# Weight preparation, two adaLN dots and a planned order around the output projection of an encoder layer

## The chip, the cores and the metric

The kernel runs on one core of one Trainium2 chip. The metric is the device time of one execution in microseconds, the median of several runs. Matmuls run on PE (TensorE, its weight loads are PEld), elementwise work on DVE (VectorE) and ACT (ScalarE), a few powers on POOL (GpSimd). SP (SyncE) issues nearly all loads from memory, and POOL issues the stores.

## The reference, cut to what matters

One layer, 1024 positions, 1024 channels, all in float32:

```python
mod = silu(c) @ w_ada + b_ada
sh1, sc1, gt1, sh2, sc2, gt2 = split(mod, 6)
h = rmsnorm(x, norm1_g) * (1 + sc1) + sh1
u, v, q, k, va, gate_a, gate_b = split(h @ w_in, cuts)
a_out = gmlp_branch(u, v, ...) @ w_a              # per chunk of 128 positions
b_out = window_attention_branch(q, k, va, ...) @ w_b
merged = sigmoid(gate_a) * a_out + sigmoid(gate_b) * b_out
x = x + gt1 * (merged @ w_o)
h2 = rmsnorm(x, norm2_g) * (1 + sc2) + sh2
f_gate, f_up = split(h2 @ w_ffn_in, 2)
x = x + gt2 * ((silu(f_gate) * f_up) @ w_ffn_out)
```

## The kernel before, in words

**Numbers.** Each float32 operand of a large product is kept as a high and a low part. A product is the sum of three products of parts (high x high, high x low, low x high). For a weight unit of 128 x 1024 a load fills a `raw` tile, ACT casts it to the high part `wh` and DVE subtracts to get the low part `wl`. `wpool` has three buffers each of `raw`, `wh` and `wl`, so the load of a unit waits until the unit three before it is no longer read. Helper functions record every operation of an engine, so nearly all rows of the profile have line 144; loads have L198 and stores L203 or L206. Rows are told apart by tile names.

**Stages.** `half(0)` and `half(1)` (L643) handle 512 positions each: q and k of the attention, v, the gMLP branch, and then a loop d = 0 to 7 over output channels with `w_a` and `w_b` (units `w_ab[d]`). `gate_products` (L1389) computes gates and `merged`, for d = 2 to 7 in a form with seven products of half the size (Strassen's), in the order of `STEPS` (L1376). `out_products` (L1518) does the product with `w_o` in the same form, adds it to x, and forms column sums of squares for the second norm. The FFN follows.

**The conditioning vector.** A row of w_ada is 512 KB, loaded as a 128 x 1024 tile. `ada_late` (L604) is one dot of it with silu(c) on DVE; after each fourth column a few small operations on `mod`. In half 0, `ada_next(2)` (L1231) does two dots in each of d = 2 and d = 3. Their tiles come out of `raw`. While half 0 runs, its loop also squares half 1's x (`sumsq`, two rows per d, on ACT with a sum into `ss` on DVE), and at the loop's d = 4 PE reads `ss` for the column sums (`col_rstd`, L374). In half 1's loop over k for q and k (L854), `ada_late` is called as often as a table of eight numbers says, on rows that `ada_load` (L629) loaded in pairs into a `mid` tile one or more k earlier. `mid` tiles rotate over eight buffers; the stores of `hd` (half 1's modulated x) read some of them.

**The gates' end.** For d = 7, steps 4 and 5 of `gate_products` also cast and split the first two units of `w_o`. The products of `out_products` need token blocks with names T1, T2, T3, T4, B11, B21, B22: sums of quarters of `merged`, each as high part (ACT) and low part (DVE), in four rows k of 128 x 512. T1 is the quarter `x0`, whose sums are done by d = 5; its four casts and four low parts were the second thing that `out_products` issued.

**A planned order.** `out_products` does not issue its work as written. Each `add` records an operation with its engine, a cost, and the names that it reads and writes, in a `Plan` (L42). `order` simulates the engines, takes at each step the operation that can start first, and then the one due earliest, and issues all operations sorted by simulated start. V is DVE, A is ACT, T is PE, D is SP's loads, G is POOL's stores. PE's and SP's order is the order of `add`; V, A and G are free within the dependencies. `free` is when each engine is taken to come free at the start:

```python
now = {e: free.get(e, 0.0) for e in queues}
...
key = (max(at, now[e] + 0.3), late[i], i)
...
plan.run({"V": 2.5, "A": 1.5, "T": 0.0})
```

**The products with w_o.** Output rows are treated in four pairs p. Each product of a pair is 12 matmuls of 512 columns. `USE` (L1615) says which weight unit and block each takes: M1 and M2 take `w_o[2p]` itself (key "0", blocks B11 and B21); T2 and T3 take a unit A of sums of w_o, T1 and B22 a unit C of sums, both from a scratch `sO` in memory in two parts; T4 takes halves of odd rows of w_o (unit B). First come all M1 and M2 (L1688), then T2, T3, T4 (L1727), then T1 and B22 (L1794). M1, T2, T3 and T4 of a pair accumulate in one PSUM bank, and between them `accumulate` (L1634) lets DVE read that bank into a row of the result. Where `(name, p)` is in `THROUGH`, ACT copies the scaled bank to a tile `t`, and DVE adds that from SBUF. `need` (L1605) and `make` (L1583) fetch, cast and split a unit; `fetch` (L1572) plans the load. `col_sums` (L1760) is behind the first T1. Two units for the FFN, `w_gate[4]` and `w_gate[5]` ("f", 0 and 1, tiles `first`), are loaded and prepared on the way.

Of the kernel before, what the change touches and what calls it, by code (L numbers as in the profile page):

```python
# [19 lines left out]
KT = D // P  # L20
# [86 lines left out]
def kernel(  # L107
# [535 lines left out]
    def half(hf):  # L643
# [102 lines left out]
        for k in range(KT):  # L746
# [97 lines left out]
            if hf == 1:  # L844

                if k in (0, 2, 4):
                    wq_raw = raw_unit(w_q[k // 2 + 1])
                if k == 2:
                    wk_raw = raw_unit(w_kv[1])
                if k == 4:  # L850
                    wk = unit(None, V, wk_raw)
                if k in (1, 3, 5):
                    wq_next = unit(None, V, wq_raw)
                for _ in range((0, 2, 2, 2, 2, 3, 3, 0)[k]):  # L854
                    ada_late(*ada_loaded.pop(0), silu_c)
                if k < 6:
                    ada_load()
# [304 lines left out]
        for d in range(KT):  # L1162
# [65 lines left out]
            if d == 4:  # L1228
                h_next.extend([[hid(), hid()], [hid(), hid()]])
            if d in (2, 3):  # L1230
                ada_next(2)  # L1231
# [157 lines left out]
    def gate_products(hH, hL):  # L1389
# [30 lines left out]
        def ready_sum(f, n):  # L1420
# [4 lines left out]
            if n == 3:  # L1425
                for i, q in enumerate((a11, a22, a12, a21)):
                    store(sF[f][:, i * HALF : (i + 1) * HALF], q)

        for d in GD:
            banks = {}  # L1430
            for i, (u, part, t, b, first) in enumerate(STEPS):
# [40 lines left out]
                if d == KT - 1:  # L1472
                    if i == 2:
                        mH, mL = [hid(), hid()], [hid(), hid()]
                    if i in (2, 3, 5):
                        for k in ((0, 1), (2, 3, 4), (), (5, 6))[i - 2]:
                            split(merged[0][k // 4][:, k % 4, :], mH[k // 4][:, k % 4, :],
                                  mL[k // 4][:, k % 4, :])
                    if i == 4:
                        oblk["T1"] = (fpt("tt1h"), fpt("tt1l"))  # L1480
                        wo_units.append(unit(w_o[0]))
                    if i == 5:
                        wo_units.append(unit(w_o[2]))
                if (d, i) == (GD[0], 5):
                    for hf in range(2):
# [13 lines left out]
                elif i == 4:  # L1499
                    V.tensor_tensor(c22, bank, c22, op=ALU.add)  # L1500
                    A.activation(c22, c22, AF.Tanh, scale=-0.5)
                    gate_low(d + 1, 0)
                elif i == 5:
                    V.tensor_tensor(v, bank, v, op=ALU.add)
                    A.activation(v, v, AF.Tanh, scale=0.5)
                elif i == 6:
                    c21 = tmp()
                    A.activation(c21, bank, AF.Tanh, scale=-0.5)
                    merge(c21, ps[1, 1])
                    V.tensor_tensor(merged[1][d // 4][:, d % 4, :], s, c21, op=ALU.add)  # L1510
                    ps = load_p(d + 1)
# [6 lines left out]
    def out_products(merged):  # L1518
# [30 lines left out]
        def blocks():  # L1549
            high("B21", m1, "m1", 3)  # L1550
            lo("B21", m1, "m1", 3)
            for k in KS:
                high("T1", x0, "x0", k)
                lo("T1", x0, "x0", k)
# [28 lines left out]
        def make(key, parts, to=None):  # L1583
            r = fetch(key, parts)
            w = to
# [11 lines left out]

        names = {}
        lo_, hi_, all_ = slice(0, HALF), slice(HALF, UNIT), slice(0, UNIT)
# [82 lines left out]

        need("0", 2)
        c11 = [stream(("xs", "hs")[p % 2]) for p in range(NPAIR)]
        for p in range(NPAIR):
            add("D", "load", lambda p=p: load(c11[p], x_rows(0, 2 * p)), [], [f"c{p}"])
        blocks()
        first = [(0, "M1"), (1, "M1"), (0, "M2"), (2, "M1"), (1, "M2"), (3, "M1"), (2, "M2"), (3, "M2")]  # L1688
        THROUGH = (('M1', 1), ('M1', 2), ('M1', 3),)
        for n, (p, name) in enumerate(first):  # L1690
# [129 lines left out]
        add("T", "few", None, ["ss"], [])  # L1820
        plan.run({"V": 2.5, "A": 1.5, "T": 0.0})
        sums.extend((sq[0], sq[1]))
# [565 lines left out]
```

## Time and profile before

| | before |
|---|---|
| median of 3 runs | 1216.77 us (1216.29 to 1217.22) |
| profiled execution, its own time | 1217.2 us |
| span of the profile | 1215.3 us |
| granted TensorE clock | 1.0 |
| PE busy | 1207.9 us (99%), 5653 instructions |
| PEld busy | 1007.1 us (83%) |
| DVE busy | 929.6 us (76%), 1505 instructions |
| ACT busy | 583.7 us (48%), 956 instructions |
| POOL busy | 154.9 us (13%) |
| moved by DMA | 241.00 MB, mean 198 GB/s |

The span is the part of the execution that has records; 1.9 us of the execution's time lie around it. Times in rows of the trace are counted from the span's start. A row of the timeline has start, duration, engine, line, operation, output <- inputs, shapes; in brackets is the idle time of that engine ahead of it and what ended it. "x2" at a row's end stands for two such instructions in a row. Half 0 lasts until about 204 us, half 1's loop for q and k is at about 205 to 238, the products with w_o run from about 501 to 581.

### The profile page before, as it was taken

The page shows a single profiled execution, that of the slowest core. Times are in us where ns is not written, and L with a number is a line of the kernel's source. Part 1 is how long each engine was busy: PE and PEld are TensorE (multiplying, and loading weights), DVE is VectorE, ACT ScalarE, POOL GpSimd, SP SyncE. Part 2 cuts the span into 40 slices and gives each one's busy share as a digit, 9 for nine tenths or more (in the row PEclk, how much of TensorE's full clock was granted, in tenths as well). Part 3 has the DMA queues.
Part 4 walks back from the last instruction along what each step waited for, and adds up shares of the span by engine and source line. Part 5 has one row for each costly group of instructions (what it writes and reads, how often), then busy time and mean ns, then how long its engine had stood idle before and what let it go on. Part 6 is the DMA issues. An engine that isn't in the chain of part 4 may idle for free.

```text
span 1215.3 us, 15658 instructions
## 1 busy us (share of the span) xinstructions
PE 1207.9 (99%) x5653; PEld 1007.1 (83%) x5653; DVE 929.6 (76%) x1505; ACT 583.7 (48%) x956; POOL 154.9 (13%) x190
## 2 busy tenths in 40 slices
PE   9999999999999999999999999999999999999998
PEld 7888888888888888878888888888888888888887
DVE  9999977789978886898987767676676765765646
ACT  5667865367855433645553333333333334433341
POOL 0024323024322000001000010010000000000001
PEclk9999999999999999999999999999999999999999
DMA  9742169653277643467313445454555449995552
GB/s 364 287 181 99 36 221 337 266 212 137 75 256 280 209 141 104 145 239 274 104 52 122 173 171 213 173 207 171 191 192 203 159 159 373 393 356 190 191 173 104
DMA packets 79457, 241.00 MB, mean 198 GB/s; under 512 B 9106, under 2 KB 9362, under 8 KB 74132
## 3 DMA queue, kind: packets, MB, share of 16 engines
q1 hardware_dynamic: 63748, 165.55, 39.3%
q0 software_dynamic: 15632, 74.46, 16.2%
q8 instruction: 44, 0.72, 0.2%
q14 instruction: 33, 0.27, 0.1%
HBM read 178.63 MB, written 61.34 MB: 197 GB/s over the span
## 4 chain that ended last, share of the span: by engine, by line
PE 93%; DMA 3%; DVE 2%; ACT 1%; issue 0%; SPq 0%; DVEq 0%; ACTq 0%
PE at L144 47%; PE mm L144 46%; DMA mid<-in_w_ada_dram 1%; DVE mid L144 1%; DMA raw<-in_w_ada_dram 1%; DMA raw<-in_w_q_dram 1%; DVE wl L144 1%; DMA mid<-in_xA_dram 0%; DVE raw L144 0%; DMA ws<-in_w_up_dram 0%; DVE ss L144 0%; DMA raw<-sO 0%; ACT wh L144 0%; ACT mid L144 0%; DVE t L144 0%
## 5 line engine op out<-in xcount | busy, mean ns | idle before, releaser
L144 ACT CAST wh<-raw 128x1024 fp32r<-128x1024 f32 (+1 forms) x154 | 157.0, 1021 | 110.0 <-PE mm L144 47.0
L144 DVE TENSOR_TENSOR wl<-raw,wh 128x1024 fp32r<-128x1024 f32 (+1 forms) x141 | 165.5, 1177 | 54.2 <-ACT wh L144 52.1
L144 PE MATMUL mm<-mid,wh 128*128 128x512 f32 x640 | 197.5, 390 | 0.2 <-DVE mid L144 0.2
L144 PEld LDWEIGHTS mm<-mid,wh 128*128 128x128 f32 x640 | 119.8, 188 | 25.2 <-DVE mid L144 0.6
L144 PE MATMUL mm<-wh,h 128*128 128x512 f32 x384 | 124.7, 397 | 0.2 <-ACT h L144 0.2
L144 PE MATMUL mm<-mid,wl 128*128 128x512 f32 x320 | 124.6, 389 | 0.0
L144 PE MATMUL mm<-h,wh 128*128 128x512 f32 x304 | 94.4, 392 | 0.0
L144 PE MATMUL at<-h,wh 128*128 128x512 f32 x304 | 93.8, 390 | 0.0
L144 PEld LDWEIGHTS mm<-wh,h 128*128 128x128 f32 x384 | 70.8, 188 | 14.0 <-ACT h L144 0.6
L144 DVE TENSOR_TENSOR wl<-ws,wh 128x1024 fp32r<-128x1024 f32 (+1 forms) x50 | 55.9, 1117 | 24.3 <-ACT wh L144 24.3
L144 PE MATMUL mm<-wl,h 128*128 128x512 f32 x192 | 71.2, 391 | 0.0
L144 PEld LDWEIGHTS mm<-mid,wl 128*128 128x128 f32 x320 | 60.1, 188 | 12.5
L144 PEld LDWEIGHTS at<-h,wh 128*128 128x128 f32 x304 | 56.9, 188 | 11.8
L144 ACT CAST wh<-ws 128x1024 fp32r<-128x1024 f32 (+1 forms) x50 | 48.3, 966 | 37.6 <-DVE ws L144 25.3
L144 PEld LDWEIGHTS mm<-h,wh 128*128 128x128 f32 x304 | 56.6, 188 | 11.6
L144 ACT ACTIVATE t<-t 128x512 f32<-128x512 f32 x46 | 28.4, 630 | 72.9 <-DVE t L144 72.9
L144 DVE TENSOR_TENSOR ol<-raw,oh 128x1024 fp32r<-128x1024 f32 x30 | 36.6, 1224 | 31.3 <-ACT oh L144 31.2
L144 PE MATMUL mm<-h,wl 128*128 128x512 f32 x152 | 59.3, 390 | 0.0
L144 PE MATMUL at<-h,wl 128*128 128x512 f32 x152 | 59.2, 389 | 0.0
L144 ACT ACTIVATE xs<-xs 128x512 f32<-128x512 f32 x21 | 13.3, 632 | 93.7 <-DVE xs L144 93.7
L144 ACT CAST oh<-raw 128x1024 fp32r<-128x1024 f32 x30 | 31.6, 1053 | 44.7 <-PE at L144 21.2
L144 PE MATMUL at<-wl,wh 128*128 128x512 f32 (+1 forms) x136 | 52.7, 388 | 0.0
(301 smaller groups left out, 2883.7 us busy)
## 6 DMA issues: line engine op xcount, KB each, us to landing
mid<-in_w_ada_dram SPq DMA_DIRECT2D x28, 512.0 KB, 7.4
raw<-in_w_gate_dram SPq DMA_DIRECT2D x26, 512.0 KB, 3.6
tA<-hid POOLq DMA_DIRECT2D x11, 1024.0 KB, 4.6
tB<-hid POOLq DMA_DIRECT2D x11, 1024.0 KB, 5.2
wo<-in_w_out_dram POOLq DMA_DIRECT2D x22, 512.0 KB, 6.1
wS<-wo POOLq DMA_DIRECT2D x11, 1024.0 KB, 5.4
raw<-wS SPq DMA_DIRECT2D x44, 256.0 KB, 3.5
raw<-tB SPq DMA_DIRECT2D x44, 256.0 KB, 4.9
```

Source lines behind the costliest of these rows:

```text
L144: ins = f(*args, **kw)
```

## The change

It has five edits. (1) In half 0, the two dots and two loads of d = 3 go, and half 1's table for k = 0 to 7 gives 16 dots in place of 14, with one more `ada_load` (at k = 6). (2) In the gates at d = 7, T1's four casts are issued at steps 4 and 5 behind those of the units of w_o, and its low parts for k = 0 and 1 behind the tanh of those steps; `out_products` only adds those for k = 2 and 3. (3) The load of `w_o[6]` is planned right behind that of `w_o[4]`, ahead of the four loads of x, and `make` later takes what is in `fetched`. (4) `("M1", 0)` joins `THROUGH`. (5) The times at which the plan takes DVE and ACT to come free are 4.9 and 3.6 in place of 2.5 and 1.5.

```diff
--- before.py
+++ after.py
@@ -851,9 +851,9 @@
                     wk = unit(None, V, wk_raw)
                 if k in (1, 3, 5):
                     wq_next = unit(None, V, wq_raw)
-                for _ in range((0, 2, 2, 2, 2, 3, 3, 0)[k]):
+                for _ in range((0, 3, 3, 2, 2, 2, 2, 2)[k]):
                     ada_late(*ada_loaded.pop(0), silu_c)
-                if k < 6:
+                if k < 7:
                     ada_load()
             sts = [(hH[k // 4][:, k % 4, t * P : (t + 1) * P], hL[k // 4][:, k % 4, t * P : (t + 1) * P])
                    for t in range(NT)]
@@ -1227,7 +1227,7 @@
                     in_order[0] = False
             if d == 4:
                 h_next.extend([[hid(), hid()], [hid(), hid()]])
-            if d in (2, 3):
+            if d == 2:
                 ada_next(2)
             if d > 4:
                 for k in ((0, 1), (2, 3, 4), (5, 6, 7))[d - 5]:
@@ -1425,6 +1425,14 @@
             if n == 3:
                 for i, q in enumerate((a11, a22, a12, a21)):
                     store(sF[f][:, i * HALF : (i + 1) * HALF], q)
+
+        def t1_high(*ks):
+            for k in ks:
+                A.copy(oblk["T1"][0][:, k, :], merged[1][0][:, k, :])
+
+        def t1_low(k):
+            h, l = oblk["T1"]
+            V.tensor_tensor(l[:, k, :], merged[1][0][:, k, :], h[:, k, :].bitcast(F32), op=ALU.subtract)
 
         for d in GD:
             banks = {}
@@ -1479,8 +1487,10 @@
                     if i == 4:
                         oblk["T1"] = (fpt("tt1h"), fpt("tt1l"))
                         wo_units.append(unit(w_o[0]))
+                        t1_high(0, 1)
                     if i == 5:
                         wo_units.append(unit(w_o[2]))
+                        t1_high(2, 3)
                 if (d, i) == (GD[0], 5):
                     for hf in range(2):
                         merged.append([midt(F32, 4)])
@@ -1500,9 +1510,13 @@
                     V.tensor_tensor(c22, bank, c22, op=ALU.add)
                     A.activation(c22, c22, AF.Tanh, scale=-0.5)
                     gate_low(d + 1, 0)
+                    if d == KT - 1:
+                        t1_low(0)
                 elif i == 5:
                     V.tensor_tensor(v, bank, v, op=ALU.add)
                     A.activation(v, v, AF.Tanh, scale=0.5)
+                    if d == KT - 1:
+                        t1_low(1)
                 elif i == 6:
                     c21 = tmp()
                     A.activation(c21, bank, AF.Tanh, scale=-0.5)
@@ -1549,8 +1563,7 @@
         def blocks():
             high("B21", m1, "m1", 3)
             lo("B21", m1, "m1", 3)
-            for k in KS:
-                high("T1", x0, "x0", k)
+            for k in (2, 3):
                 lo("T1", x0, "x0", k)
             for k in KS:
                 add("V", "v512", lambda k=k: negsum(x0[:, k, :], x1[:, k, :], x0[:, k, :]),
@@ -1581,7 +1594,7 @@
             return r
 
         def make(key, parts, to=None):
-            r = fetch(key, parts)
+            r = fetched.pop(key, None) or fetch(key, parts)
             w = to
             if to is None:
                 w = f"w{count['w'] % 3}"
@@ -1595,7 +1608,7 @@
             add("V", "v1024", lambda: split_low(tiles[key], *units[key]), [r, w + "h"], [w + "l"])
             names[key] = w
 
-        names = {}
+        names, fetched = {}, {}
         lo_, hi_, all_ = slice(0, HALF), slice(HALF, UNIT), slice(0, UNIT)
 
         def need(kind, p):
@@ -1681,12 +1694,13 @@
                 [tn], [f"x1d{hf}{d}"])
 
         need("0", 2)
+        fetched["0", 3] = fetch(("0", 3), [(all_, w_o[6])])
         c11 = [stream(("xs", "hs")[p % 2]) for p in range(NPAIR)]
         for p in range(NPAIR):
             add("D", "load", lambda p=p: load(c11[p], x_rows(0, 2 * p)), [], [f"c{p}"])
         blocks()
         first = [(0, "M1"), (1, "M1"), (0, "M2"), (2, "M1"), (1, "M2"), (3, "M1"), (2, "M2"), (3, "M2")]
-        THROUGH = (('M1', 1), ('M1', 2), ('M1', 3),)
+        THROUGH = (('M1', 0), ('M1', 1), ('M1', 2), ('M1', 3),)
         for n, (p, name) in enumerate(first):
             product(p, name)
             if n == 2:
@@ -1818,7 +1832,7 @@
             add("T", "mm", None, [f"h{x}{k}" for x in "hl" for k in range(4 * q, 4 * q + 4)]
                 + [names["g", 0] + x for x in "hl"], [])
         add("T", "few", None, ["ss"], [])
-        plan.run({"V": 2.5, "A": 1.5, "T": 0.0})
+        plan.run({"V": 4.9, "A": 3.6, "T": 0.0})
         sums.extend((sq[0], sq[1]))
         early.extend(units[k, i] for k in "fg" for i in range(2))
         raw2.append(tiles["g", 2])
```

The order of the instructions on the engines moves with it, at three places above all.

DVE in half 0, at the loop's d = 2 to 4. `ss` is the sum of squares of half 1's x, `raw,acc_mod<-raw,silu_c` is a dot, `wl` the low part of a w_ab unit, `ms` is what DVE makes of PE's column sums. Before:

```order
L144 TENSOR_TENSOR wl_2035<-raw_2032,wh_2034 128x1024
L144 SCALAR_TENSOR_TENSOR raw_2076,acc_mod<-raw_2076,silu_c 128x1024
L144 SCALAR_TENSOR_TENSOR raw_2079,acc_mod<-raw_2079,silu_c 128x1024
L144 TENSOR_TENSOR mod<-acc_mod,cc 128x4
L144 TENSOR_TENSOR ss_1931<-ss_1931,t_396_2070 128x512
L144 TENSOR_TENSOR mod<-mod,base 128x4
L144 TENSOR_TENSOR ss_1931<-ss_1931,t_397_2073 128x512
L144 TENSOR_TENSOR wl_2087<-raw_2084,wh_2086 128x1024
L144 TENSOR_SCALAR ms_2124<-at_2119 128x4
```

And of the change:

```order
L144 TENSOR_TENSOR wl_2035<-raw_2032,wh_2034 128x1024
L144 TENSOR_TENSOR wl_2079<-raw_2076,wh_2078 128x1024
L144 TENSOR_TENSOR ss_1931<-ss_1931,t_396_2070 128x512
L144 TENSOR_TENSOR ss_1931<-ss_1931,t_397_2073 128x512
L144 TENSOR_SCALAR ms_2116<-at_2111 128x4
L144 TENSOR_TENSOR wl_2129<-raw_2126,wh_2128 128x1024
```

The two dots and the two operations on `mod` behind them are gone, and the low part of the next unit, which stood behind both sums, stands ahead of them.

DVE in the products with w_o, around the sums and low parts for T3. `xs<-mm` and `mid<-mm` are readings of PSUM banks: M1(0)'s is `xs_5083<-mm_5089` before, then come T2(0)'s (of the same bank) and T2(1)'s. The rows without a bank are T3's, T4's and B22's sums and low parts, and `wl` the low parts of weight units. Before:

```order
L144 TENSOR_TENSOR wl_5225<-raw_5110,wh_5224 128x1024
L144 SCALAR_TENSOR_TENSOR mid_4610<-mid_4306,mid_4610 128x512 x4
L144 SCALAR_TENSOR_TENSOR xs_5083<-mm_5089,mod,xs_5083 128x512
L144 TENSOR_TENSOR mid_5078<-mid_4304,mid_5077 128x512 x2
L144 TENSOR_TENSOR wl_5274<-raw_5154,wh_5273 128x1024
L144 TENSOR_TENSOR mid_5078<-mid_4304,mid_5077 128x512 x2
L144 TENSOR_TENSOR wl_5294<-raw_5200,wh_5293 128x1024
L144 TENSOR_TENSOR mid_5080<-mid_4610,mid_5079 128x512
L144 SCALAR_TENSOR_TENSOR mid_5256<-mm_5089,mod,mid_5256 128x512
L144 TENSOR_TENSOR mid_5080<-mid_4610,mid_5079 128x512 x3
L144 SCALAR_TENSOR_TENSOR mid_5256<-mm_5115,mod,mid_5256 128x512
```

And of the change, where M1(0)'s sum is `xs_5088<-t_988_5134` and T2(0)'s bank `mm_5094`:

```order
L144 TENSOR_TENSOR wl_5223<-raw_5113,wh_5222 128x1024
L144 SCALAR_TENSOR_TENSOR mid_4303<-mid_4305,mid_4303 128x512 x2
L144 SCALAR_TENSOR_TENSOR mid_4609<-mid_4305,mid_4609 128x512 x4
L144 TENSOR_TENSOR mid_5083<-mid_4303,mid_5082 128x512
L144 TENSOR_TENSOR wl_5266<-raw_5154,wh_5265 128x1024
L144 TENSOR_TENSOR mid_5083<-mid_4303,mid_5082 128x512 x3
L144 TENSOR_TENSOR wl_5291<-raw_5185,wh_5290 128x1024
L144 TENSOR_TENSOR mid_5085<-mid_4609,mid_5084 128x512
L144 SCALAR_TENSOR_TENSOR mid_5269<-mm_5094,mod,mid_5269 128x512
L144 TENSOR_TENSOR mid_5085<-mid_4609,mid_5084 128x512 x3
L144 SCALAR_TENSOR_TENSOR mid_5269<-mm_5116,mod,mid_5269 128x512
L144 TENSOR_TENSOR xs_5088<-t_988_5134,xs_5088 128x512
```

The reading of M1(0)'s bank is gone from its place ahead of T3's low parts; its sum, now of a copy in SBUF, stands behind the readings of T2(0) and T2(1).

SP's loads in the products with w_o, from that of the first `w_gate` unit for "first" on. `x1d` is the scratch with the new x, `sO` that with the sums of w_o (units C here), `ws` a tile for w_up in the next stage. Before:

```order
L198 DMA raw_5472<-in_w_gate_dram 128x1024
L198 DMA mid_5301<-x1d 128x512 x2
L198 DMA raw_5481<-sO 128x512 x2
L198 DMA raw_5485<-in_w_gate_dram 128x1024
L1264 DMA ws_5763<-in_w_up_dram 128x1024
L198 DMA raw_5516<-sO 128x512 x2
L198 DMA mid_5370<-x1d 128x512 x2
L198 DMA raw_5539<-sO 128x512 x2
L198 DMA raw_5545<-sO 128x512 x2
L198 DMA raw_5571<-in_w_gate_dram 128x1024
```

And of the change:

```order
L198 DMA raw_5472<-in_w_gate_dram 128x1024
L198 DMA mid_5300<-x1d 128x512 x2
L198 DMA raw_5478<-sO 128x512 x2
L198 DMA raw_5486<-in_w_gate_dram 128x1024
L198 DMA raw_5517<-sO 128x512 x2
L198 DMA mid_5387<-x1d 128x512 x2
L198 DMA raw_5540<-sO 128x512 x2
L198 DMA raw_5546<-sO 128x512 x2
L1264 DMA ws_5764<-in_w_up_dram 128x1024
L198 DMA raw_5572<-in_w_gate_dram 128x1024
```

The load of w_up stands behind the three pairs of `sO` and one pair of `x1d` that it stood ahead of.

## The prediction

> **What bounds the kernel now.** First the page's line of busy times:
>
> ```profile
> PE 1207.9 (99%) x5653; PEld 1007.1 (83%) x5653; DVE 929.6 (76%) x1505; ACT 583.7 (48%) x956; POOL 154.9 (13%) x190
> ```
>
> PE is busy nearly all the time, and the change neither adds a matmul nor moves one. So it can only take away, or add, pauses of PE. What a pause costs isn't read from the busy time, since matmuls overlap. The chain that ended last has a stretch without pauses:
>
> ```profile
> 811.52 38.08 PE at L144 x168
> ```
>
> 168 matmuls of 512 columns in 38.08 us: 0.227 from start to start. A pause costs what the distance between two starts has above 0.227. The view of waits for PE names one kind twice (the columns: us in total, times, longest):
>
> ```profile
> PE at L144 <- DVE ss L144: 0.9, 2, 0.5
> ```
>
> So I looked at PE's timeline at these two, and in the products with w_o (501 to 581), where the change works. Start, duration, then the idle time that the view saw:
>
> ```profile
> 188.38 0.39 PE L144 MATMUL mm<-mid,wl 128*128 128x512 f32 x1
> 189.13 1.02 PE L144 MATMUL at<-ones,ss 128*128 128x1 f32 x8 [0.36 <-DVE ss L144]
> ...
> 522.70 0.39 PE L144 MATMUL at<-h,wl 128*128 128x512 f32 x1
> 523.21 0.47 PE L144 MATMUL mm<-tt2h,wh 128*128 128x512 f32 x1
> ...
> 528.51 0.39 PE L144 MATMUL mm<-tt2h,wl 128*128 128x512 f32 x1
> 529.06 0.73 PE L144 MATMUL mm<-mid,wh 128*128 128x512 f32 x2 [0.17 <-DVE mid L144]
> ...
> 558.89 0.39 PE L144 MATMUL mm<-tt1h,wl 128*128 128x512 f32 x1
> 559.80 1.05 PE L144 MATMUL at<-ones,ss 128*128 128x1 f32 x8 [0.53 <-DVE ss L144]
> ```
>
> The four pauses, each as distance minus 0.227: column sums of half 0, 0.75 - 0.23 = 0.52. T2(0) after M2(3), 0.51 - 0.23 = 0.28. T3(0) after T2(1), 0.55 - 0.23 = 0.32, and its first two matmuls take 0.73 where such a pair without a pause would take 0.39 + 0.23 = 0.62, so 0.43 in all. Column sums after T1(0), 0.91 - 0.23 = 0.68. Together **1.91 us**, which is all that the change can reach but for pauses too short to count; this ceiling is 0.16% of the time, under the 0.2% (2.43 us) that a measurement of this kernel can tell from no change.
>
> **Half 0's two dots.** DVE ahead of the first pause:
>
> ```profile
> 182.85 1.23 DVE L144 SCALAR_TENSOR_TENSOR raw<-raw,silu_c 128x1024 f32<-128x1024 f32 x1 [0.18 <-DMA raw<-in_w_ada_dram]
> ...
> 186.16 1.23 DVE L144 SCALAR_TENSOR_TENSOR raw<-raw,silu_c 128x1024 f32<-128x1024 f32 x1 [2.07 <-DMA raw<-in_w_ada_dram]
> ...
> 188.29 0.69 DVE L144 TENSOR_TENSOR ss<-ss,t 128x512 f32<-128x512 f32 x1
> ```
>
> The sum of squares stands behind two dots whose loads came late, and PE goes on when it ends (188.29 + 0.69 = 188.98). In the new order both dots and their two loads of 512 KB are gone, and the low part of w_ab[6] stands in their place. Its load is issued where the first dot's was and takes the same buffer, so I put its landing at 182.85 at the latest. ACT's cast must also wait until PE is through with the buffer of w_ab[3], which is when d = 4 begins: its two products are 24 matmuls, 24 x 0.227 = 5.44 before 188.38 + 0.23, so 183.2. Cast and low part, priced by the 1.23 of the dots above (as wide, and no shorter than either), end by 185.7. The last square is bound elsewhere:
>
> ```profile
> 185.67 0.63 ACT L144 ACTIVATE t<-mid 128x512 f32<-128x512 f32 x1 [1.19 <-DMA pd<-t]
> ```
>
> It ends at 186.3, the last sum 0.69 later, at 187.0, and PE asks at 188.61. The pause goes, with 1.6 to spare. **0.52 saved**, bounds 0 and 0.52.
>
> **The same dots in half 1.** There are 16 dots in place of 14, over k = 1 to 7. Two of them now stand ahead of the wait at k = 3. DVE's idle time there:
>
> ```profile
> 223.59 1.23 DVE L144 TENSOR_TENSOR wl<-raw,wh 128x1024 fp32r<-128x1024 f32 x1 [3.69 <-ACT wh L144]
> ...
> 237.32 1.29 DVE L144 COPY mid<-mm 128x512 f32<-128x512 f32 x2 [0.80 <-PE mm L144]
> ```
>
> Two dots, 2.46 at most by the 1.23 above, fit into 3.69 of waiting for a buffer that PE frees, so the row at 223.59 doesn't move. From there to the eviction at 237.32 the old and the new order have equally many dots (8) and low parts; each dot only uses a load made one step later. **Cost nothing**, as long as the loads keep up. The two added loads go ahead of w_v[0] on SP's queue, and w_v's loads land later by them. The DMA's load, one digit per us from 200 to 240, and the stretch where it is full (last column GB/s):
>
> ```profile
> DMA  9999999989999999999999999999787200000573
> ```
>
> ```profile
> 204.00:228.00 24.00, 24.00 (x128) 20.72 (x127) 17.27 (x29) 6.69 (x9) 1.91 (x4) 1.00 1.01 387
> ```
>
> The queue is full until about 230 and nearly empty from 231 to 237. Two loads of 512 KB at 387 GB/s are 2.7 us (an estimate from that row), so even behind all others they are in by 232.7. The last pair of dots begins at 237.32 - 0.80 less a low part and two dots of at most 1.23, so 232.8 or later. If that cover were gone, the copies of the q banks would be late, which PE needs empty for v: that is a rival below.
>
> **The products with w_o.** DVE and what it stands on (503 to 559):
>
> ```profile
> 503.21 0.69 DVE L144 SCALAR_TENSOR_TENSOR t<-t,hs 128x512 f32<-128x512 f32 x1 [0.70 <-ACT t L144]
> ...
> 522.32 0.75 DVE L144 SCALAR_TENSOR_TENSOR xs<-mm,mod,xs 128x512 f32<-128x512 f32 x1
> ...
> 528.25 0.76 DVE L144 SCALAR_TENSOR_TENSOR mid<-mm,mod,mid 128x512 f32<-128x512 f32 x1
> ...
> 557.27 0.75 DVE L144 SCALAR_TENSOR_TENSOR mid<-mm,ngt,mid 128x512 f32<-128x512 f32 x1
> 557.93 1.22 DVE L144 TENSOR_TENSOR wl<-raw,wh 128x1024 fp32r<-128x1024 f32 x1
> 559.07 0.69 DVE L144 TENSOR_TENSOR ss<-ss,t 128x512 f32<-128x512 f32 x1
> ```
>
> *Two low parts of T1 into the gates.* One costs 0.60: 0.69 as such a row of 512 lasts, less the 0.09 by which the next starts early (557.27 + 0.75 - 557.93). They go behind the add of step 4 and of step 5, where DVE waits 0.70 for ACT's tanh (the row at 503.21; the same at step 4), so they are free there, and 1.20 is gone from the end of the gates on. The four casts on ACT stand ahead of tanhs that wait for DVE anyway; ACT is the half idle engine.
>
> *M1(0) through ACT.* T2(0) adds into the bank that holds M1(0); it began when DVE had read that bank (522.32 + 0.75 = 523.07). Now ACT copies it right behind the cast for w_o[4], and DVE adds the copy later from SBUF. T2(0)'s other inputs were not what it waited for: the low part of its weights stands four sums ahead of that reading. **0.28 saved**, bounds 0 and 0.28. On DVE 0.66 (557.27 to 557.93, such a reading) leaves the stretch ahead of T3(0) and comes back as an add of 0.60 behind it.
>
> *T3(0).* It waited for the reading of T2(0)'s bank at 528.25, which was late because of what stood ahead. 1.20 + 0.66 less puts it at 526.4; T2(0) ends at 523.21 - 0.28 + 12 x 0.227 = 525.7, so the reading is free then and over by 527.2, and PE asks at 529.06 - 0.32 - 0.28 = 528.5. **0.43 saved**, bounds 0 and 0.43 (0 if a cast on ACT, now in another order, holds DVE up by more than 1.3).
>
> *w_o[6] one load earlier.* On SP it goes ahead of four loads of x, the first of which is read at 522.32, and ahead of A0's pair; it takes the raw buffer of w_o[0]. Its cast and low part move up by a few rows. M1(3) didn't wait before, so I count 0.
>
> *The last pause.* PE's column sums wait for a chain: T4(3) read by DVE (557.27), its square on ACT, the sum at 559.07, with C1's low part between; 559.80 - 557.27 = 2.53, and this order is the same after. So all hangs on when DVE can read T4(3). Its result is there at 558.89 + 0.23 - 12 x 0.227 + 0.16 (the 0.39 that a matmul lasts less 0.23) = 556.6 before, and 0.28 + 0.43 earlier after: 555.9. DVE wasn't ready then; it waited upstream for a load, w_gate[5]:
>
> ```profile
> 551.80 1.05 ACT L144 CAST first<-raw 128x1024 fp32r<-128x1024 f32 x1 [3.30 <-DMA raw<-in_w_gate_dram]
> ```
>
> ```profile
> 541.38 1.57 SPq L198 DMA_DIRECT2D mid<-x1d  x2
> 543.04 0.91 SPq L198 DMA_DIRECT2D raw<-sO  x2
> 544.28 0.33 SPq L198 DMA_DIRECT2D raw<-in_w_gate_dram  x1
> ```
>
> From that landing to the reading it took 557.27 - 551.80 = 5.47. The two reads of x1d at 541.38 wait for stores of rows that DVE finishes; DVE is 1.86 ahead, less the add of 0.60: 1.26. So the load goes out 1.3 us earlier, and up to 1.7 if the raw buffer behind it is what held it. I take 1.5: landing 550.3, DVE ready at 555.8, reading at 555.9, sums ready at 558.4, when PE asks (559.12 - 0.71 = 558.4). Left of the 0.68 is 0 to 0.1: **0.6 saved**. If the load lands as late as before, all is as late as before: the sums start at 559.8 again, and 0.28 and 0.43 are lost with the 0.68. Bounds 0 and 1.39 for the three pauses together. w_up's load, first read in the next stage, now stands behind three sO pairs and not ahead of them, so C1 to C3 don't come later by it.
>
> [...] Going by the median of such loads on the page there would be 3.9 us more:
>
> ```profile
> raw<-in_w_gate_dram SPq DMA_DIRECT2D x26, 512.0 KB, 3.6
> ```
>
> [...]
>
> **The sum.** 0.52 + 0.28 + 0.43 + 0.6 = 1.83 us. The profiled execution took 1217.2 with a span of 1215.3, so 1.9 lie around; it would take 1215.4. It is the slowest of the three shown; from their median, 1216.77, the forecast is **1214.9**. Chance 0.64.
>
> **The rivals.** *The load of w_gate[5] doesn't come earlier.* Then w_o gives nothing, half 0's 0.52 stays: 1216.3; with some of it, up to 1215.7. For it speaks that three transfers stand ahead of the load and POOL's stores beside it; against it, that everything that triggers these moves forward. Chance 0.22.
>
> *The change doesn't do what it says.* The free times are numbers of a planning table; if ACT's casts in the new order hold DVE up at T2 and T3, and the square in half 0 comes late, the pauses stay where they are: 1216.8. Chance 0.06.
>
> *Slower: half 1's added pair lands late.* It takes the buffer of half 0's second block of x, which must have been stored to memory. SP has waited long for such a store before in the same stage (us in total, times, longest):
>
> ```profile
> SPq L198 <- DMA hd<-mid: 10.6, 2, 9.4
> ```
>
> Behind the pair's dots stand on DVE a low part and the copies of two q banks, and PE's first v products need these banks. With 1.3 for the last dot and 1.2 for the low part, PE waits once the landing is past 237.32 - 2.5 = 234.8. I expect it by 232.7. With 9.4 more it is 242.1 and PE waits 7.3: 1216.8 - 1.8 + 7.3 = 1222.3. It decides the sign from 1.8 us of pause on, a landing past 236.6. Against it: the pair comes behind four others on SP, and those long waits lay ahead of the first of these. Chance 0.08. [...]
>
> **How the numbers follow.** Likeliest 1214.9. The range takes in the forecast with 1.0 below it for short pauses and the scatter of the median, and the rival without w_o's gain: 1213.9 to 1216.9. Faster by over 0.2% needs the whole ceiling and half a us more: 0.13, out of the forecast's 0.64. Slower by over 0.2%: 0.08. The rest, 0.79, is within.
>
> **What would show it.** Right: PE's column sums start 0.23 to 0.3 behind the matmul ahead of them, near 188.6 and 557.9; T2(0) and T3(0) start without a gap; DVE's read of T2(0) stands near 526. Wrong: ACT's second cast of "first" still at 551 or later; DVE idle on a w_ada load near 233; a gap of PE at the first v product.

## The result, and the profile after

The changed kernel takes **1215.05 us** (median of 18 runs, 1214.72 to 1216.11), the kernel before 1217.14 us in as many runs beside it. The ratio is 0.9985 with a 95% interval of 0.9978 to 0.9992: 2.1 us less, 1.0 to 2.7 by the interval. So 18 runs of each can tell this gain from none, though it lies under the 2.43 us that the prediction took for the least that can be told. Forecast were 1.83 us less and a time of 1214.9. The profiled execution has a span of 1212.9 us, 2.4 less than before.

The page's line of busy times, and PE's waits (the columns: us in total, times, longest):

```profile
PE 1206.6 (99%) x5653; PEld 1006.9 (83%) x5653; DVE 929.4 (77%) x1505; ACT 584.3 (48%) x957; POOL 156.2 (13%) x190
```

```profile
PE at L144 <- DVE identr L144: 1.9, 1, 1.9
PE at L144 <- DVE mid L144: 0.2, 1, 0.2
PE mm L144 <- ACT h L144: 0.2, 1, 0.2
```

Busy times say nothing, as before: no engine lost work worth naming. What is new is what is missing: the kind that was named twice before, PE waiting for `ss`, is gone. PE's timeline at the four places of the prediction:

```profile
188.24 0.39 PE L144 MATMUL mm<-mid,wl 128*128 128x512 f32 x1
188.47 0.95 PE L144 MATMUL at<-ones,ss 128*128 128x1 f32 x8
...
521.76 0.39 PE L144 MATMUL at<-h,wl 128*128 128x512 f32 x1
521.99 0.39 PE L144 MATMUL mm<-tt2h,wh 128*128 128x512 f32 x1
...
527.20 0.39 PE L144 MATMUL mm<-tt2h,wl 128*128 128x512 f32 x1
527.43 0.61 PE L144 MATMUL mm<-mid,wh 128*128 128x512 f32 x2
...
557.12 0.39 PE L144 MATMUL mm<-tt1h,wl 128*128 128x512 f32 x1
557.37 1.05 PE L144 MATMUL at<-ones,ss 128*128 128x1 f32 x8
```

All four distances are 0.23 to 0.25, so all four pauses are gone. The same rows show where the 2.4 us come from, if each start is taken from that of the same matmul before:

| row | before | after | lead |
|---|---|---|---|
| last matmul ahead of half 0's column sums | 188.38 | 188.24 | 0.14 |
| half 0's column sums | 189.13 | 188.47 | 0.66 |
| last matmul ahead of T2(0) | 522.70 | 521.76 | 0.94 |
| T2(0) | 523.21 | 521.99 | 1.22 |
| last matmul of T2(1) | 528.51 | 527.20 | 1.31 |
| T3(0) | 529.06 | 527.43 | 1.63 |
| last matmul of T1(0) | 558.89 | 557.12 | 1.77 |
| column sums behind it | 559.80 | 557.37 | 2.43 |

The lead grows by 0.52, 0.28, 0.32 and 0.66 at the four pauses, together 1.78. The rest is small steps between: 0.14 ahead of everything that the change touches (a difference of two executions), 0.28 from half 0 to T2(0), 0.09 and 0.14 behind T2(0) and T3(0).

### The profile page after: what moved, and what is told of

The parts are those of the page before. It is cut to its first block, busy times and chain, and to the rows that moved or that the text cites. A ratio compares the mean times of both kernels' runs of the same rounds, so it can differ in the third digit from the quotient of the medians.

```text
span 1212.9 us, 15658 instructions
## 1 busy us (share of the span) xinstructions
PE 1206.6 (99%) x5653; PEld 1006.9 (83%) x5653; DVE 929.4 (77%) x1505; ACT 584.3 (48%) x957; POOL 156.2 (13%) x190
## 4 chain that ended last, share of the span: by engine, by line
PE 98%; DMA 0%; DVE 0%; ACT 0%; issue 0%; SPq 0%; DVEq 0%; ACTq 0%
PE mm L144 50%; PE at L144 48%; DMA mid<-in_xA_dram 0%; DVE mid L144 0%; ACT mid L144 0%; ACT wh L144 0%; ACT h L144 0%; ACT silu_c L144 0%; DVE crow L144 0%; ACT mod L144 0%; DVE zeros L144 0%; DVE ones L144 0%; SPq L198 0%; DVE identr L144 0%; DVEq L144 0%
```

## Experiments

Two theories were to be told apart. **The sum**, as forecast: each pause has a cause of its own, and each edit takes its own away. **The whole**: the edits to the products with w_o work only together, and one alone gains little or loses. All runs below but the first two have one time only, which can't tell 0.2 to 1 us; there PE's pauses in the profile are compared.

### Edit 1 alone, and edits 2 to 5 alone

```diff
 e1_dots (kernel before)
-                for _ in range((0, 2, 2, 2, 2, 3, 3, 0)[k]):
+                for _ in range((0, 3, 3, 2, 2, 2, 2, 2)[k]):
-                if k < 6:
+                if k < 7:
-            if d in (2, 3):
+            if d == 2:
```

> The kernel before with edit 1 alone: two dots and their loads from half 0's d = 3 to half 1. By the sum (each pause of PE goes with its own cause): the distance at half 0's column sums falls from 0.75 us to 0.23 to 0.30, PE has no new pause in half 1 between 204 and 245 us, and the pauses of 0.28, 0.43 and 0.68 in the products with w_o stay; the time falls by 0.5 us. By the rival that the added loads or dots cost half 1 something: a pause of over 0.2 us near the copies of the q banks (236 to 240 us), and no gain. By the rival that all of the change's gain lies in the products with w_o: no difference.

> The kernel before with edits 2 to 5, without edit 1. By the sum: half 0's pause of 0.52 us stays, the three pauses in the products with w_o go, and the time falls by 1.3 to 1.7 us. By the rival that one of the places works through the other: either the pauses in the products with w_o stay in part (a fall under 1.0), or the fall is the whole 2.1.

Edit 1 alone took 1216.46 us (12 runs; before 1217.36; ratio 0.9992, 0.9983 to 1.0001), edits 2 to 5 alone 1215.52 us (11 runs; ratio 0.9986, 0.9977 to 0.9994). The falls of 0.9 and 1.8 are near the forecast 0.5 and 1.3 to 1.7; by their intervals the first can't be told from none. PE's timeline is sharper. Edit 1 alone, at the column sums of half 0 and those behind T1(0):

```profile
188.37 0.39 PE L144 MATMUL mm<-mid,wl 128*128 128x512 f32 x1
188.59 0.95 PE L144 MATMUL at<-ones,ss 128*128 128x1 f32 x8
...
557.95 0.39 PE L144 MATMUL mm<-tt1h,wl 128*128 128x512 f32 x1
559.04 0.94 PE L144 MATMUL at<-ones,ss 128*128 128x1 f32 x7 [0.70 <-DVE ss L144]
```

Half 0's pause is gone, and half 1 has no new one. But the pause behind T1(0) is 1.09 - 0.23 = 0.86 in place of 0.68. In this execution T2(0) happened to start without a gap, and what PE gained there it waited for later: the last sums were as late as ever. Edits 2 to 5 alone, at half 0's column sums:

```profile
188.38 0.39 PE L144 MATMUL mm<-mid,wl 128*128 128x512 f32 x1
188.99 1.02 PE L144 MATMUL at<-ones,ss 128*128 128x1 f32 x8 [0.22 <-DVE ss L144]
```

That pause stays (0.38), and those in the products with w_o are all gone. So edit 1 and the rest are independent, as the sum has it. Half 0's pause isn't a fixed 0.52: in the six profiles with the old dots it was 0.52, 0.38, 0.67, 0.55, 0.46 and once below 0.1, as the second row's load came.

### One edit taken out of the changed kernel

```diff
 e4_old_free (changed kernel)
-        plan.run({"V": 4.9, "A": 3.6, "T": 0.0})
+        plan.run({"V": 2.5, "A": 1.5, "T": 0.0})
 e5_no_through (changed kernel)
-        THROUGH = (('M1', 0), ('M1', 1), ('M1', 2), ('M1', 3),)
+        THROUGH = (('M1', 1), ('M1', 2), ('M1', 3),)
 e6_no_t1 (changed kernel; t1_high and t1_low no longer called)
-            for k in (2, 3):
+            for k in KS:
+                high("T1", x0, "x0", k)
                 lo("T1", x0, "x0", k)
 e7_no_w6 (changed kernel)
-        fetched["0", 3] = fetch(("0", 3), [(all_, w_o[6])])
```

> The changed kernel with the plan's old free times (2.5 and 1.5). In the order that comes out of it three low parts of T4 and the sum of M1(0) stand ahead of DVE's reading of T2(0) that stood behind it: 3 x 0.60 + 0.60 = 2.4 us later, so at 527.6, done at 528.4, when PE asks for T3(0) at 527.4. By the theory that the order is what the free times buy: a pause of 0.8 to 1.1 us ahead of T3(0), T2(0) without one. By the rival that the table's numbers don't matter and the work taken off does it all: no pause at either.

> The changed kernel without edit 4: DVE reads M1(0)'s bank itself. By the prediction's step (the copy by ACT is what saves the pause ahead of T2(0)): a pause of 0.2 to 0.3 us there. By the rival that T1's two low parts in the gates suffice: this reading now comes right behind T4's sums, which end at 519.9 in the changed kernel, so the bank is free at 520.7, 1.3 us ahead of T2(0) (522.0), and there is no pause; the reading of T2(0) comes at 525.3 and T3(0) has none either.

> The changed kernel without edit 2: T1's four casts and four low parts all behind the gates again. DVE is 1.2 us later up to T3. By the rival of the run without edit 4 (each of the two edits covers for the other): no pause ahead of T2(0), the reading of T2(0)'s bank is over at 525.22 + 0.75 + 1.2 = 527.2, just ahead of T3(0) at 527.4, so none or under 0.1 us there. By the prediction's step (1.2 us is needed for T3(0)): 0.1 to 0.4 ahead of T3(0). At the column sums behind T1(0), where the changed kernel has no margin, 0 to 0.4 by both.

> The changed kernel without edit 3: w_o[6] is loaded behind the four rows of x again, and w_up's load goes ahead of C1 to C3's pairs. DVE's and ACT's orders are the same as in the changed kernel. By the prediction (M1(3) doesn't wait, the load ahead is worth 0): no pause at M1(3) or T2. By the rival that what edit 3 buys is w_up's place on SP: C1's pair lands up to 1.3 us later, C1's low part stands ahead of the last sum of squares, and the column sums behind T1(0) get a pause of 0.3 to 1.0 us.

| run | one time, us | pause at T3(0) | at T1(0) | at the column sums |
|---|---|---|---|---|
| without the new free times | 1215.90 | 0.90 + 0.11 | 0 | 0 |
| without the copy of M1(0) | 1215.60 | 0 | 0 | 0 |
| without T1 in the gates | 1219.17 | 0.55 + 0.11 | 0.2 and 0.9 | 2.1 |
| without w_o[6] ahead | 1219.12 | 0.57 + 0.11 | 0 | 1.2 |

(The kernel before took 1217.36 beside the first and 1216.73 beside the others. T2(0) had no pause in any. The 0.11 is what the matmuls right behind the pause were late in addition.)

*Free times*: T3(0) starts at 527.97, 1.13 behind the matmul ahead of it, so it waits 0.90, within the 0.8 to 1.1 worked out from the order of DVE (the profile names DVE's `mid` as what PE waited for). The order is what the two numbers buy.

*Copy of M1(0)*: in the order of the changed kernel T2(0) doesn't need it. DVE's reading of M1(0)'s bank is over at 521.13, 1.3 ahead of T2(0), as the rival of this run has it.

*T1 in the gates and w_o[6] ahead*: without either, all that the change gained in the products with w_o is lost, and more. None of my bounds had that. DVE and ACT without w_o[6] ahead, and SP's loads behind which it then stands:

```profile
512.75 1.23 DVE L144 TENSOR_TENSOR wl<-raw,wh 128x1024 fp32r<-128x1024 f32 x1 [1.90 <-ACT wh L144]
```

```profile
511.66 1.05 ACT L144 CAST wh<-raw 128x1024 fp32r<-128x1024 f32 x1 [2.05 <-DMA raw<-in_w_o_dram]
```

```profile
499.57 0.33 SPq L198 DMA_DIRECT2D hs<-in_xA_dram  x1
505.41 0.33 SPq L198 DMA_DIRECT2D xs<-in_xA_dram  x1
...
506.30 0.38 SPq L198 DMA_DIRECT2D raw<-in_w_o_dram  x1
```

Between 499.57 and 505.41 SP waits to issue a row of x, and w_o[6] goes out only at 506.30. With the new order its cast stands early on ACT and its low part early on DVE, so both engines stand still for 2 us, and all behind them comes later. The changed kernel issued the same load by 496.97, behind w_o[4]'s and ahead of the rows of x:

```profile
483.61 13.36 SPq L198 DMA_DIRECT2D raw<-in_w_o_dram  x4
```

The rival named for the run without w_o[6] ahead held in part, too. w_up's load went out ahead of C1's pair again, at 550.79, and ACT and DVE waited for that pair right ahead of the last sum:

```profile
557.23 1.05 ACT L144 CAST wh<-raw 128x1024 fp32r<-128x1024 f32 x1 [1.13 <-DMA raw<-sO]
```

```profile
558.31 1.23 DVE L144 TENSOR_TENSOR wl<-raw,wh 128x1024 fp32r<-128x1024 f32 x1 [0.82 <-ACT wh L144]
```

So up to 0.8 of the 1.2 at the column sums may come from w_up's place; the run doesn't separate the two.

Without T1 in the gates, DVE is late by those low parts and some waits. The two stores behind which the reads of x1d wait go out 2.2 later than in the changed kernel, the reads 4.3 and w_gate[5]'s load 4.4 (546.45 in place of 542.02). Why the reads follow the stores 2 us later than there stays open. The cast of w_gate[5]:

```profile
553.77 1.05 ACT L144 CAST first<-raw 128x1024 fp32r<-128x1024 f32 x1 [4.52 <-DMA raw<-in_w_gate_dram]
```

In the changed kernel this cast stands 4.7 earlier (its row is shown below).

### One edit put into the kernel before

```diff
 e8_free_only (kernel before)
-        plan.run({"V": 2.5, "A": 1.5, "T": 0.0})
+        plan.run({"V": 4.9, "A": 3.6, "T": 0.0})
 e9_w6_only (kernel before; make() pops what is fetched)
+        fetched["0", 3] = fetch(("0", 3), [(all_, w_o[6])])
```

> The kernel before with edit 5 alone, the two numbers. In its order the reading of M1(0)'s bank stands where it stood, behind the same work, and T2(0)'s reading stands one low part (0.6 us) earlier. By the theory that order and work taken off both count: T2(0) keeps its pause of 0.28, T3(0)'s 0.43 goes to 0 to 0.1, the column sums' 0.68 changes little. By the rival that the numbers alone bring the gain: all three pauses go.

> The kernel before with edit 3 alone. DVE's and ACT's orders are as before, only SP's differs: w_o[6] goes out at about 497 in place of 506. By the theory from the runs without one edit (w_o[6]'s late load holds ACT's cast by 0.29 us and DVE by 0.22 in the kernel before, and by more in every order that wants it earlier): these two waits go, the 0.28 ahead of T2(0) falls to 0 to 0.1, T3(0)'s 0.43 and the column sums' 0.68 stay within 0.2 of what they were. By the prediction's step (worth 0): all as before.

The two numbers alone: 1225.53 us, 8.8 slower than the kernel before beside it. Neither theory had that. It is the same wait again, in the new order and with the old load:

```profile
511.41 1.05 ACT L144 CAST wh<-raw 128x1024 fp32r<-128x1024 f32 x1 [1.80 <-DMA raw<-in_w_o_dram]
```

DVE stood still for 2.11 behind it, read M1(0)'s bank at 523.80, and PE waited at T2(0), at T1(0) and at the column sums, 2.2, 1.9 and 2.1 us. (At T2(0) the profile names a cast on ACT, which ended at 524.63; DVE's reading ended at 524.54, so the two lie too close to be told apart by it. Ahead of T1(0), ACT's cast of w_gate[5] waited 5.25 for its load.)

```profile
522.22 0.39 PE L144 MATMUL at<-h,wl 128*128 128x512 f32 x1
524.69 0.47 PE L144 MATMUL mm<-tt2h,wh 128*128 128x512 f32 x1 [2.08 <-ACT mid L144]
```

w_o[6]'s load ahead, alone, changes no order on DVE or ACT. T2(0) starts 0.23 behind the matmul ahead of it:

```profile
522.43 0.39 PE L144 MATMUL at<-h,wl 128*128 128x512 f32 x1
522.66 0.45 PE L144 MATMUL mm<-tt2h,wh 128*128 128x512 f32 x1
```

ACT's and DVE's waits of 0.29 and 0.22 are gone, as expected, and the other pauses are 0.31 and 0.61 (1216.73 us, one execution; the kernel before took 1218.84 beside this run and beside the last three below).

This run alone doesn't show that the load made the 0.28, since three other profiles with the old load and the old order up to T2(0), e1, e3 and e10, had less than 0.1 there as well. But in those three ACT's cast of w_o[6] waited less than 0.1 for its load; only the profile with the pause has the wait of 0.29. And in all five T2(0) starts 0.14 to 0.17 behind the end of M1(0)'s reading. So the reading left no margin, as the prediction had it, and a load that was late in one execution used up what there was.

### w_gate[5]'s load

```diff
 e3_f1_early, e10_f1_early_free (kernel before)
                 make(("f", 0), [(all_, w_gate[EARLY - 2])], "f0")
+                make(("f", 1), [(all_, w_gate[EARLY - 1])], "f1")
 ...
             elif n == 9:
-                make(("f", 1), [(all_, w_gate[EARLY - 1])], "f1")
 e3_f1_early only: the last sum is held behind C1's low part
-                    [q], ["ss"])
+                    [q] + ([names["C", 1] + "l"] if (hf, d) == (0, 7) else []), ["ss"])
```

> The kernel before with one thing changed: w_gate[5]'s load goes on SP right behind w_gate[4]'s, ahead of the two reads of x1d and of C0's pair; the last sum of squares is held behind C1's low part, as it stands before. No DVE work is taken from ahead of it. By the theory that this load sets the last pause: ACT's second cast of first moves from 551.8 to 549 us or earlier, DVE reads T4(3) as soon as PE has it (556.6), and the distance at the column sums behind T1(0) falls from 0.91 to 0.23 to 0.35 us, while T2(0) and T3(0) keep their pauses of 0.28 and 0.43. By the rival that DVE's own work ahead sets it (1.2 us of T1, the copy of M1(0)): the distance stays near 0.9.

> As the run with w_gate[5]'s load right behind w_gate[4]'s, without the hold on the last sum, which the planner then puts ahead of C1's low part. By the theory that the load set when DVE could read T4(3), and that in the held run the sum only waited for C1's cast: DVE reads T4(3) at 556.5 as in the held run, the square follows, the sum ends 0.75 + 0.63 + 0.7 = 2.1 later, at 558.6 to 558.8, and the distance at the column sums is 0.23 to 0.4 in place of 0.91. By the rival that something else holds the sums: over 0.6 still. An order without C1's low part ahead, but with the late load, would give 2.53 - 1.14 + 0.7 or so: a distance of about 0.5.

In the held run (1218.08 us, one execution) ACT's second cast of `first` ended at 549.26, and DVE read T4(3) at 556.43 as soon as PE had it, as expected; but the column sums waited 1.8. My hold made that: ACT does the square of T4(3) ahead of C1's cast, and the sum had to wait for C1's low part behind that cast. So the first half of the theory stood and the run couldn't show the second. Without the hold (1216.07 us, one execution), ACT, DVE and PE:

```profile
546.28 1.98 ACT L144 CAST first<-raw 128x1024 fp32r<-128x1024 f32 x2
```

```profile
555.44 0.75 DVE L144 SCALAR_TENSOR_TENSOR mid<-mm,ngt,mid 128x512 f32<-128x512 f32 x1 [0.23 <-PE mm L144]
556.95 0.69 DVE L144 TENSOR_TENSOR ss<-ss,t 128x512 f32<-128x512 f32 x1 [0.76 <-ACT t L144]
```

```profile
557.73 0.39 PE L144 MATMUL mm<-tt1h,wl 128*128 128x512 f32 x1
557.96 0.72 PE L144 MATMUL at<-ones,ss 128*128 128x1 f32 x6
...
585.10 1.02 PE L144 MATMUL at<-ones,ss 128*128 128x1 f32 x8 [0.61 <-DVE ss L144]
```

The pause is gone, and DVE reads T4(3) as soon as PE has it, so the load no longer decides. It isn't the load alone: in this run's order C1's low part also stands behind the last sum and not ahead of it, which by the expectation would bring the distance to about 0.5 even with the late load. And the next column sums, 27 us later, now wait 0.61, where the view saw no wait in the kernel before:

```profile
586.36 0.80 PE L144 MATMUL at<-ones,ss 128*128 128x1 f32 x6
```

From T1(0)'s last matmul to these sums the run took 585.10 - 557.73 = 27.37, the kernel before 586.36 - 558.89 = 27.47: of the 0.68 only 0.1 was kept. What gave it back is the next load, the pair of sO behind C1's. ACT and DVE wait for it, and DVE reads a bank of T1 late:

```profile
560.61 1.05 ACT L144 CAST wh<-raw 128x1024 fp32r<-128x1024 f32 x1 [2.74 <-DMA raw<-sO]
```

```profile
561.69 1.23 DVE L144 TENSOR_TENSOR wl<-raw,wh 128x1024 fp32r<-128x1024 f32 x1 [1.83 <-ACT wh L144]
562.83 0.74 DVE L144 SCALAR_TENSOR_TENSOR mid<-mm,ngt,mid 128x512 f32<-128x512 f32 x1
```

From that reading to the column sums DVE works nearly without a break. In the changed kernel, where w_up's load stands behind these pairs, the cast comes at 557.18, and the same reading waits for PE only:

```profile
561.31 0.75 DVE L144 SCALAR_TENSOR_TENSOR mid<-mm,ngt,mid 128x512 f32<-128x512 f32 x1 [1.52 <-PE mm L144]
```

Nothing was given back there. No run moves w_up's load alone.

### How much cover half 1 has

```diff
 e11_dots18_spread, e12_dots18_late (changed kernel)
-            if d == 2:
-                ada_next(2)
+                for _ in range((2, 3, 3, 2, 2, 2, 2, 2)[k]):    (spread)
+                for _ in range((0, 3, 3, 2, 2, 2, 2, 4)[k]):    (late)
-                if k < 7:
-                    ada_load()
+                for _ in range((2, 1, 1, 1, 1, 1, 1, 0)[k]):
+                    ada_load()
```

> The changed kernel with the two dots of half 0's d = 2 moved to half 1 as well: 18 dots there (2, 3, 3, 2, 2, 2, 2, 2 for k = 0 to 7), one more pair of loads at k = 0. It asks how much cover half 1 has left. In the changed kernel DVE still has 2.50 us of idle time at 222.87 and the last pair of rows landed at 229.6, 2.6 ahead of its first dot at 232.2. Two more dots (2.3) early fit into the 2.50, one more MB of loads (2.6 us) uses up the 2.6. By the theory of the prediction (dots are free while DVE waits for a buffer and the loads keep up): no pause of PE over 0.2 at 236 to 245 us. By the rival that the queue is full and each added load is paid: a pause of 0.5 to 2.6.

> The same 18 dots and the same loads with the two added ones at the end (0, 3, 3, 2, 2, 2, 2, 4). DVE's idle time ahead of the copies of the q banks was 0.80 in the changed kernel; two dots of 1.14 put the copies 1.5 us later. By the theory that cover is a matter of the place: PE waits ahead of the first v products for DVE's copies, 0.5 to 1.5 us, where the run with the same dots early has none. By the rival that only the loads count: the same pause in both.

Spread (1215.64 us, one execution): no pause in half 1. DVE's idle time that the early dots used was 2.50 in the changed kernel and is 0.47:

```profile
222.97 1.23 DVE L144 TENSOR_TENSOR wl<-raw,wh 128x1024 fp32r<-128x1024 f32 x1 [0.47 <-ACT wh L144]
```

Late (1217.03 us, one execution): PE waits at the first v product.

```profile
239.01 0.50 PE L144 MATMUL mm<-wl,h 128*128 128x512 f32 x1 [0.99 <-DVE wl L144]
```

1.27 us with the 0.11 behind it, in the range expected. What PE waits for first is not a q bank, as I had put it, but the low part of v's first weights, which stands ahead of these copies. The loads were the same in both, so the place decides.

## Why the prediction was right, and where its steps were not

**What bounds, and the ceiling**: right. All that was gained at the named places are the four pauses: 1.78 and 0.14 in the table, of the 1.91 counted.

**Half 0** (0.52): right in place, size and timing. ACT and DVE in the changed kernel:

```profile
183.00 1.05 ACT L144 CAST wh<-raw 128x1024 fp32r<-128x1024 f32 x1 [1.19 <-PE mm L144]
```

```profile
184.09 1.23 DVE L144 TENSOR_TENSOR wl<-raw,wh 128x1024 fp32r<-128x1024 f32 x1 [1.50 <-ACT wh L144]
185.23 1.48 DVE L144 TENSOR_TENSOR ss<-ss,t 128x512 f32<-128x512 f32 x2
```

The cast waits for PE until 183.0 (worked out: 183.2), the low part ends at 185.3 (185.7), and the sums at 186.7 (187.0), while PE asks at 188.5.

**Half 1** (nothing): right. The reading of the q banks stands 0.80 behind DVE's last work as it did before, and two further dots were free in the right place.

**T2(0)** (0.28, by M1(0)'s copy through ACT): the pause went, but not by the copy, since without it there was none either. It is right that T2(0) starts when M1(0)'s bank has been read. But in the order of before that left a pause above 0.1 in one profile of four, the one in which w_o[6]'s load was late; its trace had the row, a wait of 0.22 on DVE ahead of w_o[6]'s low part. I priced what stood next to the pause and not what stood ahead of it. The copy alone, in the kernel before, wasn't run.

**w_o[6] one load earlier** (0): wrong. "M1(3) didn't wait before, so I count 0" looked only at PE. DVE and ACT ran their work in the order of issue in these traces, so a unit whose cast stands early holds up everything behind it: in the run without w_o[6] ahead ACT's cast waited 2.05 for the load and DVE's low part 1.90 for the cast. In the new order the load of 506 is worth the whole gain in the products with w_o and more: the run without it lost it, and the two numbers without it cost 8.8 us. In part the edit may also work through w_up's place on SP, which the prediction named and priced at nothing.

**T1 in the gates** (1.20 us off DVE): right that it is needed, too small in price. The 1.20 was counted against T3(0) only; without the edit the pauses were 0.55, 0.2 and 0.9, and 2.1, since the reads of x1d, and w_gate[5]'s load behind them, came later too.

**The last pause** (0.6, by w_gate[5]'s load): right. In the changed kernel:

```profile
539.98 0.97 SPq L198 DMA_DIRECT2D mid<-x1d  x2
541.04 0.89 SPq L198 DMA_DIRECT2D raw<-sO  x2
542.02 0.38 SPq L198 DMA_DIRECT2D raw<-in_w_gate_dram  x1
```

```profile
549.04 1.05 ACT L144 CAST first<-raw 128x1024 fp32r<-128x1024 f32 x1 [2.01 <-DMA raw<-in_w_gate_dram]
```

```profile
554.83 0.75 DVE L144 SCALAR_TENSOR_TENSOR mid<-mm,ngt,mid 128x512 f32<-128x512 f32 x1 [0.22 <-PE mm L144]
555.50 1.22 DVE L144 TENSOR_TENSOR wl<-raw,wh 128x1024 fp32r<-128x1024 f32 x1
556.63 0.69 DVE L144 TENSOR_TENSOR ss<-ss,t 128x512 f32<-128x512 f32 x1
```

The load goes out 2.26 earlier than before, of which PE brought 0.94 along (the lead ahead of T2(0)): 1.3 of its own, forecast 1.5. With the same 0.94 added, the other times of the working come out within 0.4: the cast at 550.0 (550.3), DVE's reading at 555.8 (555.9), the sums at 558.3 (558.4). From issue to cast the load takes 7.0 (542.02 to 549.04), before it took 7.5 (544.28 to 551.80), and the median of such loads is 3.6: an earlier issue moved this load and hardly shortened it, so of the 3.9 by that median 0.5 was seen. In both kernels four loads of 256 KB stand right ahead of it on its own queue and two stores of POOL go out meanwhile; the traces don't show what makes the 7.0. The 0.22 for the rival of a load that comes no earlier was an estimate of mine. DVE now waits for PE at T4(3) (0.22), so the load no longer decides, and the sums end at 557.32, just as PE asks (557.35). There is no margin left: the two runs with more dots had 0.27 and 0.18 there again.

So the sum of 1.83 came out near the measured 2.1 although three of its prices were wrong: the ceiling of 1.91 bounded them all, and the whole was taken. That is part luck. The 1.91 is the count of one execution, in which T2(0)'s pause was there and half 0's was near its usual size, and 0.4 of the 2.4 us between the two profiles are small steps that no edit was shown to make. That the edits depend on each other, the theory of the whole, holds for 2, 3 and 5; edit 1 adds by itself, and edit 4 wasn't needed. Edit 2 alone, and edits 3 and 5 together without the others, weren't run. Why w_o[6]'s load was in time in some executions of the old order and late in another stays open.

## What to carry to other kernels

Where engines work in order, as ACT and DVE do in these traces, the price of a late load is not the wait of its reader alone but that of everything queued behind its cast (without w_o[6] ahead 2.05 us of waiting on ACT, and pauses of PE of 0.68 and 1.2 us later on), so a new order and the loads that it wants earlier are one change: look for the load's place on its queue first. Where one engine is busy all the time, add up its pauses before anything else, since they bound every edit; and a pause that goes by one earlier load can come back a little later, when the next load is as late as ever. Work hidden in idle time has to be put where the idle time is: the same two dots were free early and cost 1.3 us late.

## What the runs showed of the hardware

Three pauses of PE, of 2.2, 2.1 and 1.2 us in two runs, were followed by half its clock. In the run with the new free times alone, around T2(0), the granted clock was 0.50 from 526.01 to 529.42. That stretch, behind as long a one ahead of it (the last three columns: clock, DMA share, GB/s):

```profile
522.60:526.01 3.41, 1.33 (x7) 1.13 (x7) 3.41 (x6) 3.41 (x6) 0.00 (x0) 1.00 0.29 74
526.01:529.42 3.41, 3.41 (x10) 2.67 (x9) 3.41 (x6) 0.09 (x1) 0.00 (x0) 0.50 0.98 311
```

Behind a pause of 2.2 us eight matmuls came 0.43 apart in place of 0.23, for 3.4 us: 1.6 us lost on top, and about as much in such a stretch behind the column sums (granted clock 0.50 from 567.00 to 570.30). The run without w_o[6] ahead has one too, behind a pause of 1.2:

```profile
558.61:562.02 3.41, 2.37 (x15) 1.82 (x14) 2.35 (x4) 0.68 (x2) 0.91 (x2) 1.00 0.99 378
562.02:565.43 3.41, 3.41 (x10) 2.63 (x9) 1.23 (x1) 1.10 (x2) 0.67 (x1) 0.50 0.94 336
```

Other pauses as long, 1.8 in the held run and 2.1 in the one without T1 in the gates, had no such stretch: the granted clock was 1.00 from 559 to 566 and from 558.4 to 565. Which pauses are followed by one, these runs don't show. In the sums above the slow stretches made the runs with one edit taken out or put in look up to 3.2 us dearer than their pauses (an estimate, twice the 1.6).
